# Low parts of 16 weight tiles of the second expert layer, made during the first layer's last sums and kept in DRAM

## The chip, the cores and the metric

The kernel runs on one NeuronCore of a Trainium2 chip. The metric is the time on the device of one execution, in microseconds (us). Of three runs the median was 2067.51 us (2065.51 to 2068.57). The profile is of one further execution, which took 2073.28 us.

## The reference, cut to what matters

256 tokens of width 1024 pass through two blocks. Each block is a token mixer and then an expert layer with 128 x 128 experts; the expert layer is the part that the change touches:

```python
def peer_2(xn, w_q, sub_keys, u_tab, v_tab):       # the first layer has the same shape
    q = (t @ w_q).reshape(n_tok, PEER_HEADS, 2, PEER_HALF)
    sc = jnp.einsum("thpk,hpnk->thpn", q, sub_keys)
    s_top, i_top = lax.top_k(sc, PEER_TOPK)         # 16 of 128, twice per head
    cand = s_top[:, :, 0, :, None] + s_top[:, :, 1, None, :]
    best, pos = lax.top_k(cand.reshape(n_tok, PEER_HEADS, kk), PEER_TOPK)
    g = jax.nn.softmax(best, axis=-1)
    act = jax.nn.gelu(einsum(u_tab[idx], t))        # chosen experts only
    return einsum(g * act, v_tab[idx])
```

Everything is float32. The kernel computes the products of all 16384 experts densely and multiplies by a gate that is zero for experts that were not chosen.

## The kernel before, in words

**Weights come as tiles of 128 x 1024 float32 (512 KB).** `plan` lists all tiles of the program in the order of their use; `fetch_to` loads them from SyncE's queue (SP) into three buffers named raw, at most three tiles ahead of the tile prepared last. A prepared tile is in two parts: `high` copies it on ScalarE (ACT) to a rounded format (whi, line 96), and `low` subtracts that copy on VectorE (DVE) to get the rest (wlo, line 103). Both parts have three buffers; `take` prepares two tiles ahead. TensorE (PE) then makes 24 matmuls for a tile, three for each of eight slices: high part by the high input, high part by the low input, low part by the high input (lines 137 to 139). The order of the instructions of every engine is the order of the program text; nothing reorders them.

**Whole tiles.** A tile marked "own" isn't split. It is loaded into three buffers of its own (rawf) and multiplied in float32 (line 131): 8 matmuls, each of which the trace records twice. In either expert layer ten of the tiles of `down` are whole: 5, 8, ..., 32.

**An expert layer** (`peer`) runs through five stages. (1) The lead: four tiles of the query weights (lead 0 to 3) are multiplied before the norm is known, while DVE and ACT make the norm; then one query tile and the first tile of `down`, q4 and S0, are multiplied together, slice by slice, as the normed input arrives (`norm_steps`). The keys (1 MB) are loaded here, between the preparation of q4 and that of S0 (line 1121). (2) Routing: the other queries q5 to q15 and the tiles S1 to S33 alternate on PE, and DVE works through the two top-16 searches, the decoding and the softmax, some 2 us behind each tile of `down` (a list of work items with estimated costs). The stage ends when DVE has written K and PE transposes it (line 1168); S32 and S33 stand behind the transposes. (3) The rest of the first 64 tiles of `down`, beside the gates. (4) The sums: for expert tile i of `up`, `weights(i + 1)` splits the gated activations (wh on ACT, line 122; wl on DVE, line 123), the tile i + 2 is prepared, and PE makes 24 matmuls (lines 1382 to 1384). Up to i = 47 a tile of `down` stands between two of `up`; from i = 48 on there are sums alone. (5) `finish` adds the result to x.

**Beside the last sums** of the first layer, from i = 66 on, the generator `before1` makes one step in each i. I call i - 65 the turn. Turns 1 to 5 make small sums and load the row crow; turn 7 works on crow (lines 315 to 317) and loads the first of eight rows aw; turns 9, 11, ..., 23 each multiply a row aw on DVE (`ada`, line 330) and load the next one, into the same single buffer.

Of the kernel before, what the change touches and what calls it, by code (L numbers as in the profile page):

```python
# [1 line left out]

# [6 lines left out]
F32 = _mybir.dt.float32  # L9
F32R = _mybir.dt.float32r  # L10
# [10 lines left out]
KT = 8  # L21
# [3 lines left out]
N0 = 34  # L25
# [26 lines left out]
class Net:  # L52
    def __init__(self, tc, a, out):
        self.tc, self.nc, self.a, self.out = tc, tc.nc, a, out
        self.items = []
        self.fetched = self.prepped = self.taken = 0

    def v(self, name, j=0, n=1):
# [23 lines left out]
    def high(self, n):  # L82

        it = self.items[n]
        if isinstance(it[3], tuple):
            return
        self.fetch_to(n + 1)
        if it[2]:
            it[3] = it[3],
            return  # L90
        if it[4]:
            hi, lo = self.extra
        else:
            hi = self.stream.tile([128, KT, 128], F32R, name="whi", bufs=3)
            lo = self.stream.tile([128, KT, 128], F32R, name="wlo", bufs=3)
        self.nc.scalar.copy(hi, it[3])  # L96
        it[3] = it[3], hi, lo

    def low(self, n):
        it = self.items[n]  # L100
# [5 lines left out]
    def prep_to(self, n):  # L106
        while self.prepped < min(n, len(self.items)):
            self.high(self.prepped)
            self.low(self.prepped)
            self.prepped += 1  # L110
            self.fetch_to(self.prepped + RAW)

    def take(self, key, index, prep=PREP):
        n = self.taken
        it = self.items[n]
        assert it[:2] == [key, index], (it[:2], key, index)
        self.prep_to(n + prep + 1)
        self.taken += 1
        return it[3]
# [918 lines left out]
            out.append(("U", n))  # L1038
        return out

    def plan_peer(self, wq, down, up):
        for st in self.peer_steps():
            if st[0] in ("q", "lead"):
                self.plan(wq, st[1], spare=st == ("lead", 1))
            elif st[0] in "SERH":

                self.plan(down, st[1], whole=4 < st[1] < N0 and st[1] % 3 == 2 and "own")
            elif st[0] == "U":
                self.plan(up, st[1], spare=st[1] == NK - 1)

    def peer(self, wq, keys, down, up, gelu, g, shift, before, finish):
        tc, nc, a = self.tc, self.nc, self.a
        steps = self.peer_steps()
        with self.sbuf("pk") as pk, self.psum("ps", 2) as self.pp, self.psum("pacc", 1) as pacc, \
# [8 lines left out]
            def S(i):  # L1063
                return self.proj(down, i, *([h] if self.items[self.taken][2] else [self.hh, self.hl]))

            with self.sbuf("rt") as rt:
# [8 lines left out]
                q = {}  # L1075
# [37 lines left out]
                lead = [acc[j].rearrange("p b t -> p (b t)")[:, :W] for j in range(4)]  # L1113
# [43 lines left out]
                n = 6  # L1157
# [46 lines left out]
            with self.sbuf("dn") as dn:  # L1204
# [3 lines left out]
                def gated(i):  # L1208
                    wf = X2[:, i - N1]
                    nc.vector.tensor_mul(wf, wf, acts.pop(i))  # L1210
# [3 lines left out]
                with self.sbuf("og") as og:  # L1214
# [89 lines left out]
                    first = []  # L1304
# [24 lines left out]
                    for m in range(ng + LAG):  # L1329
                        if m < ng:  # L1330
                            ahead_hots = one_hots(m + 2)
                            next(ahead_hots, None)
                            pool, tag = (self.pm, "sm") if m % 2 else (self.pp, "mm")
# [24 lines left out]
                        pass  # L1358
                n += N1 - N0 + RING + HELD + 1

                with self.sbuf("ga") as ga:
                    def act(i, ps):
                        g = ga.tile([128, T], F32, name="ge", bufs=2)
                        nc.scalar.activation(g, ps, gelu)
                        acts[i] = g
                        gated(i)

                    def weights(i):
                        if i >= NK:
                            return None  # L1370
                        wf = X1[:, i] if i < N1 else X2[:, i - N1]
                        wh = ga.tile([128, T], F32R, name="wh", bufs=2)
                        wl = ga.tile([128, T], F32R, name="wl", bufs=2)
                        self.split(wh, wl, wf)
                        return wh, wl

                    def bank(d):
                        return acc[d % 4][:, d // 4]

                    def spread_up(i, d, hi, lo, wh, wl):  # L1380
                        o = bank(d)
                        nc.tensor.matmul(o, hi[:, d], wh, start=i == 0 and d < 4, stop=False, skip_group_check=True)  # L1382
                        nc.tensor.matmul(o, hi[:, d], wl, start=False, stop=False, skip_group_check=True)  # L1383
                        nc.tensor.matmul(o, lo[:, d], wh, start=False, stop=i == NK - 1, skip_group_check=True)  # L1384

                    waiting = list(acts)
                    for i in held:
                        act(i, held[i])
                    w = weights(0)
                    for kind, i in steps[n:]:  # L1390
                        if waiting:
                            gated(waiting.pop(0))
                            if not waiting:
                                nc.gpsimd.dma_start(self.x, xk)
                        if kind == "S":
                            act(i, S(i))
                            continue
                        if i == N1 + 1:
                            x1.__exit__(None, None, None)
                            more = before()  # L1400
                        if i > N1 + 1:
                            next(more, None)
                        wc, w = w, weights(i + 1)
                        if i < NK - 2:
                            hi, lo = self.take(up, i)
                            for d in range(8):
                                spread_up(i, d, hi, lo, *wc)
                        elif i == NK - 2:
                            before_last = (*self.take(up, i), *wc)
                            self.prep_to(self.taken + 3)  # L1410
                        else:

                            hi, lo = self.take(up, i, prep=0)
                            for d in range(10):
                                if d < 8:
                                    spread_up(i - 1, d, *before_last)
                                if d > 1:
                                    spread_up(i, d - 2, hi, lo, *wc)
                                    finish(d - 2, bank(d - 2))

    def build(self):
        tc, nc, a = self.tc, self.nc, self.a
        self.plan_mixer1()
        self.plan_peer("w_query", "down", "up")
        self.plan_mixer2()
        self.plan_peer("w_query2", "down2", "up2")
        with tc.manual_schedule(), tc.tile_pool(name="const", bufs=1) as const, \
                tc.tile_pool(name="stream", bufs=2) as self.stream, \
                tc.tile_pool(name="np", bufs=1) as self.np, \
                tc.tile_pool(name="pm", bufs=2, space=PSUM) as self.pm:  # L1430
# [85 lines left out]
            def both_sums():  # L1516
# [5 lines left out]
                while True:  # L1522
# [1 line left out]

            self.mixer1(constants)
            self.peer("w_query", "keys", "down", "up", AF.Gelu, self.g1, self.mod[:, 24:32],
                      before1, first)
            self.mixer2(both_sums, g2)
            self.peer("w_query2", "keys2", "down2", "up2", AF.Gelu_apprx_tanh, self.v("norm2", 0, 8), None,
                      before2, second)  # L1530
# [91 lines left out]
```

## Time and profile before

| | |
|---|---|
| median of three runs | 2067.51 us |
| profiled execution, its span | 2073.28 us, 2071.5 us |
| busy: PE, DVE, ACT | 2002.1 us (97%), 1526.6 us (74%), 1057.1 us (51%) |
| one split of a tile: copy on ACT, subtraction on DVE | 1047 ns, 1224 ns, 599 of each |
| one split of gated activations: ACT, DVE | 404 ns, 422 ns, 256 of each |
| moved by DMA | 376.63 MB, 182 GB/s over the span |

In the profile PE, DVE and ACT are the shares of the span in which the engines were busy, DMA is the mean busy share of the 16 DMA engines, and a busy PE isn't PE at its peak, since matmuls overlap. The first expert layer ends at about 1025 us of the span, the lead of the second at about 1250, its routing at 1383.5.

### The profile page before, as it was taken

The page shows a single profiled execution, that of the slowest core. Times are in us where ns is not written, and L with a number is a line of the kernel's source. Part 1 is how long each engine was busy: PE and PEld are TensorE (multiplying, and loading weights), DVE is VectorE, ACT ScalarE, POOL GpSimd, SP SyncE. Part 2 cuts the span into 40 slices and gives each one's busy share as a digit, 9 for nine tenths or more (in the row PEclk, how much of TensorE's full clock was granted, in tenths as well). Part 3 has the DMA queues.
Part 4 walks back from the last instruction along what each step waited for, and adds up shares of the span by engine and source line. Part 5 has one row for each costly group of instructions (what it writes and reads, how often), then busy time and mean ns, then how long its engine had stood idle before and what let it go on. Part 6 is the DMA issues. An engine that isn't in the chain of part 4 may idle for free. (4 is left out here: it accounts for less than half of the span.)

```text
span 2071.5 us, 41220 instructions
## 1 busy us (share of the span) xinstructions
PE 2002.1 (97%) x16640; PEld 1955.9 (94%) x16640; DVE 1526.6 (74%) x3007; ACT 1057.1 (51%) x1986; POOL 51.9 (3%) x52
## 2 busy tenths in 40 slices
PE   5999999999999999999999999999999999999998
PEld 4888898999999999999999999999999999999998
DVE  7997899999655555665687779999996555555555
ACT  3453434666544444544575554446655444444444
POOL 3021000000000000000000010000000000000000
PEclk7999999999999999999999999999999999999999
DMA  8755444444555555675545564444445555555553
GB/s 300 261 203 185 161 164 153 143 142 141 198 190 186 184 186 191 209 243 190 184 153 183 183 215 172 155 153 143 143 144 201 185 184 187 189 185 186 190 184 123
DMA packets 102720, 376.63 MB, mean 182 GB/s; under 512 B 11648, under 2 KB 12032, under 8 KB 101504
## 3 DMA queue, kind: packets, MB, share of 16 engines
q1 hardware_dynamic: 101520, 369.38, 51.3%
q0 software_dynamic: 576, 4.19, 0.5%
q8 instruction: 130, 2.13, 0.4%
q14 instruction: 62, 0.51, 0.1%
q10 hardware_dynamic: 432, 0.41, 0.1%
HBM read 370.80 MB, written 3.15 MB: 181 GB/s over the span
## 5 line engine op out<-in xcount | busy, mean ns | idle before, releaser
L103 DVE TENSOR_TENSOR wlo<-raw,whi 128x1024 fp32r<-128x1024 f32 x599 | 732.4, 1224 | 248.6 <-ACT whi L96 247.3
L96 ACT CAST whi<-raw 128x1024 fp32r<-128x1024 f32 x599 | 626.4, 1047 | 238.8 <-PE acc L138 102.5
L1382 PE MATMUL acc<-wh,whi 128*128 128x256 f32 x2032 | 569.3, 280 | 2.1 <-DVE x L1494 2.1
L1384 PE MATMUL acc<-wh,wlo 128*128 128x256 f32 x2032 | 567.7, 279 | 2.2 <-DVE wlo L103 2.2
L1383 PE MATMUL acc<-wl,whi 128*128 128x256 f32 x2032 | 568.0, 280 | 1.7 <-DVE wl L123 1.3
L139 PE MATMUL mm<-hh,wlo 128*128 128x256 f32 x1880 | 530.0, 282 | 12.2 <-DVE wlo L103 12.2
L137 PE MATMUL mm<-hh,whi 128*128 128x256 f32 x1880 | 535.4, 285 | 3.3 <-ACT gg L879 1.4
L138 PE MATMUL mm<-hl,whi 128*128 128x256 f32 x1880 | 529.0, 281 | 2.9 <-DVE hl L258 2.1
L1384 PEld LDWEIGHTS acc<-wh,wlo 128*128 128x128 f32 x2032 | 381.9, 188 | 2.6 <-DVE wlo L103 2.6
L1382 PEld LDWEIGHTS acc<-wh,whi 128*128 128x128 f32 x2032 | 381.2, 188 | 2.4 <-DVE x L1494 2.3
L1383 PEld LDWEIGHTS acc<-wl,whi 128*128 128x128 f32 x2032 | 380.5, 187 | 3.0 <-DVE wl L123 2.9
L139 PEld LDWEIGHTS mm<-hh,wlo 128*128 128x128 f32 x1880 | 358.1, 190 | 16.0 <-DVE wlo L103 15.8
L137 PEld LDWEIGHTS mm<-hh,whi 128*128 128x128 f32 x1880 | 354.6, 189 | 6.4 <-ACT gg L879 1.8
L138 PEld LDWEIGHTS mm<-hl,whi 128*128 128x128 f32 x1880 | 356.0, 189 | 4.6 <-DVE hl L258 2.5
L122 ACT CAST wh<-X 128x256 fp32r<-128x256 f32 x256 | 103.4, 404 | 229.2 <-PE acc L1384 229.2
L137 PE MATMUL acc<-hh,whi 128*128 128x256 f32 x736 | 216.3, 294 | 0.0
L138 PE MATMUL acc<-hl,whi 128*128 128x256 f32 x736 | 205.3, 279 | 0.0
L139 PE MATMUL acc<-hh,wlo 128*128 128x256 f32 x736 | 204.8, 278 | 0.0
L123 DVE TENSOR_TENSOR wl<-X,wh 128x256 fp32r<-128x256 f32 x256 | 108.1, 422 | 89.1 <-ACT wh L122 89.1
L137 PEld LDWEIGHTS acc<-hh,whi 128*128 128x128 f32 x736 | 139.1, 189 | 0.0
L138 PEld LDWEIGHTS acc<-hl,whi 128*128 128x128 f32 x736 | 139.0, 189 | 0.0
L139 PEld LDWEIGHTS acc<-hh,wlo 128*128 128x128 f32 x736 | 138.4, 188 | 0.0
(343 smaller groups left out, 2136.3 us busy)
## 6 DMA issues: line engine op xcount, KB each, us to landing
raw<-in_up_dram SPq DMA_DIRECT2D x256, 512.0 KB, 3.4
raw<-in_down_dram SPq DMA_DIRECT2D x236, 512.0 KB, 3.2
raw<-in_w_in_dram SPq DMA_DIRECT2D x71, 512.0 KB, 3.3
aw<-in_w_ada_dram SPq DMA_DIRECT2D x48, 512.0 KB, 4.6
raw<-in_w_query_dram SPq DMA_DIRECT2D x32, 512.0 KB, 3.3
rawf<-in_down_dram SPq DMA_DIRECT2D x20, 512.0 KB, 4.4
rawf<-in_w_in_dram SPq DMA_DIRECT2D x10, 512.0 KB, 4.6
raw<-in_w_out_dram SPq DMA_DIRECT2D x8, 512.0 KB, 3.8
```

What stands on the lines that cost most here:

```text
L96: self.nc.scalar.copy(hi, it[3])
L103: self.nc.vector.tensor_sub(lo, raw, hi.bitcast(F32))
L122: self.nc.scalar.copy(hi, src)
L123: self.nc.vector.tensor_sub(lo, src, hi.bitcast(F32))
L137: nc.tensor.matmul(ps, hi[:, k], xh[:, k], start=k == 0 and clear, stop=False, skip_group_check=True)
L138: nc.tensor.matmul(ps, hi[:, k], xl[:, k], start=False, stop=False, skip_group_check=True)
L139: nc.tensor.matmul(ps, lo[:, k], xh[:, k], start=False, stop=k == KT - 1, skip_group_check=True)
L1382: nc.tensor.matmul(o, hi[:, d], wh, start=i == 0 and d < 4, stop=False, skip_group_check=True)
L1383: nc.tensor.matmul(o, hi[:, d], wl, start=False, stop=False, skip_group_check=True)
L1384: nc.tensor.matmul(o, lo[:, d], wh, start=False, stop=i == NK - 1, skip_group_check=True)
```

## The change

In the second layer no tile is whole any more. The low parts of 16 of its tiles (lead 0 to 3, q4, S0 and the ten that were whole) are made during the last sums of the first layer, from turn 1 on: a tile is loaded, copied to a high part on ACT and subtracted on DVE in place, and the difference is stored by a DMA from ACT's queue to a buffer in DRAM. Each tile takes two steps of the new generator, one for the copy (and the store of the tile before), one for the subtraction; a step is made in turns 1 to 7 and from then on in every odd turn. The load of a tile stands one step before its copy for the first, and beside the copy of the tile before for the others. In the second layer these 16 tiles are loaded and copied to a high part as the others are, and the low part is a load from DRAM on SP's queue instead of the subtraction on DVE.

```diff
@@ high(self, n)
         self.nc.scalar.copy(hi, it[3])
-        it[3] = it[3], hi, lo
+        if n in self.early:
+            self.nc.sync.dma_start(lo.bitcast(F32), self.early[n])
+            it[3] = hi, lo
+        else:
+            it[3] = it[3], hi, lo
+    def lows_ahead(self, pool, home, items):
+        nc = self.nc
+        raws, done = {}, None
+        def load(m):
+            if m < len(items):
+                key, index = self.items[items[m]][:2]
+                raws[m] = pool.tile([128, KT, 128], F32, name="early", bufs=3)
+                nc.sync.dma_start(raws[m], self.a[key][index])
+        load(0)
+        for m, n in enumerate(items):
+            yield
+            load(m + 1)
+            raw = raws.pop(m)
+            hi = pool.tile([128, KT, 128], F32R, name="ehi", bufs=1)
+            nc.scalar.copy(hi, raw)
+            if done:
+                nc.scalar.dma_start(*done)
+            yield
+            nc.vector.tensor_sub(raw.bitcast(F32R), raw, hi.bitcast(F32))
+            self.early[n] = home.tile([128, KT, 128], F32, name=f"lo{n}")
+            done = self.early[n], raw
+        nc.scalar.dma_start(*done)
@@ plan_peer(self, wq, down, up, first)
+            if not first and (st[0] == "lead" or st in (("q", 4), ("S", 0))
+                              or st[0] == "S" and 4 < st[1] < N0 and st[1] % 3 == 2):
+                self.ahead.append(len(self.items))
-                self.plan(down, st[1], whole=4 < st[1] < N0 and st[1] % 3 == 2 and "own")
+                self.plan(down, st[1], whole=first and 4 < st[1] < N0 and st[1] % 3 == 2 and "own")
@@ peer(...), the last sums
                         if i == N1 + 1:
                             x1.__exit__(None, None, None)
                             more = before()
+                            lows, turn = iter(()), 0
+                            if home:
+                                lows = self.lows_ahead(later.enter_context(self.sbuf("el")), home, self.ahead)
                         if i > N1 + 1:
                             next(more, None)
+                            turn += 1
+                            if turn % 2 or turn < 8:
+                                next(lows, None)
                         wc, w = w, weights(i + 1)
```

## Rows read from the trace of the kernel before

**Rows 1.** Busy time by stretch: engines with instructions, granted TensorE clock, DMA share, GB/s.
```profile
1250.50:1383.40 132.90, 127.91 (x967) 122.70 (x965) 131.96 (x491) 52.77 (x89) 0.00 (x0) 1.00 0.47 167
1240.00:1245.00 5.00, 5.00 (x33) 4.93 (x32) 3.91 (x10) 2.57 (x5) 0.00 (x0) 0.72 0.46 157
849.00:869.00 20.00, 19.69 (x168) 19.48 (x166) 13.25 (x31) 11.39 (x17) 0.00 (x0) 1.00 0.60 211
869.00:916.00 47.00, 45.87 (x383) 45.20 (x384) 34.34 (x50) 21.80 (x32) 0.00 (x0) 1.00 0.81 261
920.00:1020.00 100.00, 100.00 (x852) 100.00 (x851) 58.34 (x72) 48.06 (x71) 0.00 (x0) 1.00 0.54 188
8.00:18.00 10.00, 5.25 (x32) 5.16 (x32) 6.99 (x6) 5.61 (x13) 8.39 (x3) 0.63 1.01 405
```

**Rows 2.** Groups of instructions by line and form, routing of the second layer, 1250.5 to 1383.4.
```profile
L103 DVE TENSOR_TENSOR wlo<-raw,whi 128x1024 fp32r<-128x1024 f32 x31 | 37.6, 1214 | 0.0
...
L131 PE MATMUL mm<-h,rawf 128*128 128x256 f32 x144 | 32.6, 379 | 0.0
```

**Rows 3.** The chain that ended last, at the end of that routing: start, duration, what.
```profile
1384.30 3.46 PE mm L131 x16
1387.76 0.12 PE mm L137
...
1390.59 0.12 PE acc L137
```

**Rows 4.** PE in order of time in the second lead: start, duration, what, [idle before].
```profile
1238.42 0.39 PE L139 MATMUL mm<-hh,wlo 128*128 128x256 f32 x1 [0.76 <-DVE wlo L103]
...
1240.18 0.41 PE L137 MATMUL mm<-hh,whi 128*128 128x256 f32 x1
1240.40 0.41 PE L138 MATMUL mm<-hl,whi 128*128 128x256 f32 x1
...
1245.47 0.39 PE L138 MATMUL mm<-hl,whi 128*128 128x256 f32 x1 [0.34 <-DVE hl L261]
```

**Rows 5.** ACT in the same lead: copies of lead 2 and 3, q4, S0.
```profile
1227.00 1.98 ACT L96 CAST whi<-raw 128x1024 fp32r<-128x1024 f32 x2
1229.94 1.05 ACT L96 CAST whi<-raw 128x1024 fp32r<-128x1024 f32 x1 [0.96 <-PE acc L138]
...
1236.07 1.04 ACT L96 CAST whi<-raw 128x1024 fp32r<-128x1024 f32 x1
```

**Rows 6.** SP's queue in the same lead.
```profile
1229.32 5.35 SPq L79 DMA_DIRECT2D raw<-in_down_dram  x3
1234.72 0.42 SPq L1121 DMA_DIRECT2D keys<-in_keys_dram  x1
```

**Rows 7.** PE in order of time in the first layer's last sums.
```profile
869.35 0.39 PE L1383 MATMUL acc<-wl,whi 128*128 128x256 f32 x1 [0.66 <-DVE wl L123]
...
910.43 0.39 PE L1383 MATMUL acc<-wl,whi 128*128 128x256 f32 x1 [0.27 <-DVE wl L123]
```

**Rows 8.** DVE in the same sums: crow in turn 7, first and last of eight aw.
```profile
867.74 1.23 DVE L317 SCALAR_TENSOR_TENSOR crow<-aw,crow 128x1024 f32<-128x1024 f32 x1 [2.17 <-ACT crow L316]
...
872.33 1.23 DVE L330 SCALAR_TENSOR_TENSOR aw<-aw,crow 128x1024 f32<-128x1024 f32 x1 [0.42 <-DMA aw<-in_w_ada_dram]
...
914.41 1.23 DVE L330 SCALAR_TENSOR_TENSOR aw<-aw,crow 128x1024 f32<-128x1024 f32 x1 [0.35 <-DMA aw<-in_w_ada_dram]
```

**Rows 9.** ACT in the same sums, turns 6 and 7.
```profile
862.96 0.41 ACT L122 CAST wh<-X 128x256 fp32r<-128x256 f32 x1 [1.47 <-PE acc L1384]
...
865.55 1.06 ACT L315 ACTIVATE aw<-crow 128x1024 f32<-128x1024 f32 x1 [1.24 <-DMA crow<-in_c_dram]
```

**Rows 10.** Loads of crow on SP's queue there.
```profile
860.33 0.63 SPq L311 DMA_DIRECT2D crow<-in_c_dram  x1
```

**Rows 11.** From issue to landing: raw at 920 to 1020, aw at 869 to 916.
```profile
DMA to landing us min/median/max: 3.1/3.2/4.9
DMA to landing us min/median/max: 3.2/4.5/5.4
```

More of the change, by code (lines that the diff above doesn't have):

```diff
@@ L1 @@
+import contextlib
 import numpy as _np
@@ L55, in __init__ @@
         self.items = []
+        self.early = {}
         self.fetched = self.prepped = self.taken = 0
@@ L1039, in peer_steps, with plan_peer @@
         return out
-    def plan_peer(self, wq, down, up):
+    def plan_peer(self, wq, down, up, first):
         for st in self.peer_steps():
+            if not first and (st[0] == "lead" or st in (("q", 4), ("S", 0))
+                              or st[0] == "S" and 4 < st[1] < N0 and st[1] % 3 == 2):
+                self.ahead.append(len(self.items))
             if st[0] in ("q", "lead"):
@@ L1045, in plan_peer, with peer @@
             elif st[0] in "SERH":
-                self.plan(down, st[1], whole=4 < st[1] < N0 and st[1] % 3 == 2 and "own")
+                self.plan(down, st[1], whole=first and 4 < st[1] < N0 and st[1] % 3 == 2 and "own")
             elif st[0] == "U":
                 self.plan(up, st[1], spare=st[1] == NK - 1)
-    def peer(self, wq, keys, down, up, gelu, g, shift, before, finish):
+    def peer(self, wq, keys, down, up, gelu, g, shift, before, finish, home=None):
         tc, nc, a = self.tc, self.nc, self.a
@@ L1359, in peer @@
                 n += N1 - N0 + RING + HELD + 1
-                with self.sbuf("ga") as ga:
+                with self.sbuf("ga") as ga, contextlib.ExitStack() as later:
                     def act(i, ps):
@@ L1423, in build @@
         self.plan_mixer1()
-        self.plan_peer("w_query", "down", "up")
+        self.ahead = []
+        self.plan_peer("w_query", "down", "up", True)
         self.plan_mixer2()
-        self.plan_peer("w_query2", "down2", "up2")
+        self.plan_peer("w_query2", "down2", "up2", False)
         with tc.manual_schedule(), tc.tile_pool(name="const", bufs=1) as const, \
+                tc.tile_pool(name="lows", bufs=1, space=bass.MemoryType.DRAM) as lows, \
                 tc.tile_pool(name="stream", bufs=2) as self.stream, \
@@ L1526, in build @@
             self.peer("w_query", "keys", "down", "up", AF.Gelu, self.g1, self.mod[:, 24:32],
-                      before1, first)
+                      before1, first, lows)
             self.mixer2(both_sums, g2)
```

## The prediction

> **What bounds the kernel now.** I began with the busy time by stretch, since one share over the whole span mixes stages. In the second layer's routing DVE is busy 131.96 of 132.90 us and PE 127.91 [rows 1]: DVE ends that stage, and PE has 4.99 us to spare. In the last sums of the first layer it is the other way round: at 920 to 1020 us PE is busy all the time, DVE 58.34 of 100 us and ACT 48.06, with the DMA engines at 0.54 [rows 1]. Just before that, while the rows aw are worked on, PE already loses time (45.87 of 47.00) and DMA is at 0.81 and 261 GB/s [rows 1]. The groups by line then say what DVE does in the routing: 31 subtractions of 1214 ns for the split tiles, and none for the whole ones, of which PE has 144 records, nine tiles of 16 [rows 2]. The chain shows what PE pays for one whole tile, 3.46 us (1384.30 to 1387.76), and for the split tile after it, 24 matmuls from 1387.76 to 1390.59, 2.83 us [rows 3].
>
> **Part 1: no whole tiles in the routing.** PE saves 3.46 - 2.83 = 0.63 us a tile, 5.7 us for the nine in the routing. But whole tiles cost DVE nothing, and the new ones cost it nothing either: its 31 subtractions and all its search work remain. Nine tiles faster on PE only make PE wait longer for DVE. The gain is at most DVE's own idle time, 132.90 - 131.96 = 0.94 us, and I take 0. If the low parts from DRAM came late by 1 us each, PE would use 9 of the 4.99 + 5.7 = 10.7 us that it then has; no cost either. ACT gets ten copies of 1.05 us, beside 52.77 us busy of 132.90; ten loads of 0.524 MB add 39 GB/s to 167. The tenth whole tile, S32, stands behind the transposes, where the chain is on PE [rows 3]: -0.6 us, between -0.7 and 0.
>
> **Part 2: the lead of the second layer.** Six subtractions of about 1.22 us go. Five of them cost PE nothing. That of S0 does: PE waited 0.76 us for it, until 1238.42 [rows 4], as its copy began only at 1236.07 [rows 5]. In its place stands a load, and the question is when it lands. SP's queue before had three loads of raw from 1229.32 on and then the keys at 1234.72 [rows 6], each raw waiting for DVE's subtraction of an older tile. Now a raw waits for a copy only, so the queue moves up: raw S0 at about 1228.0, where the first of two copies from 1227.00 ends, low part 3, raw S1 at 1229.0, low part of q4, raw S2 at 1231.0 (the copy of 1229.94 plus 1.05) [rows 5], the keys, and behind them the low part of S0. That is 6 x 0.524 + 1.05 = 4.19 MB. With nothing else on the queue a raw lands 3.2 us after its issue [rows 11]; 0.524 MB at the 405 GB/s that the engines moved at share 1.01 [rows 1] are 1.3 us of it, which leaves 1.9. So the low part of S0 lands at 1228.0 + 1.9 + 4.19/0.405 = 1240.2, or at 1243.0 with 322 GB/s (261 at share 0.81, scaled to 1 [rows 1]). PE is 1.8 to 4.6 us later there than before, minus the 0.34 that it lost later in waiting for DVE's hl at 1245.47 [rows 4] and as much for the earlier gaps: DVE makes the normed input earlier now. Routing starts when PE has finished the pair and S1, so this shifts everything behind it. If the engines serve the queue otherwise and the load lands by 1237.4, PE gains about 1 us there and another at hl: -2. I take +2.0, between -2 and +5.
> The clock matters here too. In 1240 to 1245, after PE had waited, the granted clock was 0.72, with matmuls 0.22 us apart (1240.18 to 1240.40) instead of 2.83/24 = 0.118 [rows 1, 3, 4]. Of two levels, 2.4 and 1.2 GHz, that is 2.8 of 5 us at the lower, and 1.4 us lost. A longer wait brings this again, or somewhat more; it is inside the upper end.
> The Trainium skill ("DMA: Bandwidth & Descriptors", Specifications) gives about 358 GB/s as the limit of a core's HBM. By it the low part of S0 would land at 1241.6 and the term would be 1.4 us larger, an estimate. The trace differs, 405 GB/s over 10 us [rows 1], and the trace decides.
>
> **Part 3: the work beside the last sums of the first layer.** Added are 16 loads and 16 stores of 0.524 MB, 16 copies of 1.05 us on ACT, 16 subtractions of 1.22 us on DVE. PE takes 2.83 us for one i.
> Turns 1 to 8. ACT is idle 1.47 us before each wh [rows 9], which waits for PE; a copy fits in if its tile has landed. But the loads of the first tiles are issued only one or two turns ahead. The first one stands right behind a raw, as crow does at 860.33 in turn 5 [rows 10]; it lands 3.2 to 4.0 us on, then come the copy 1.05, wh 0.41, wl 0.42 and some 0.2 between them: 5.3 to 6.1 us, where PE wants wl after two i, 5.7. With two later copies I take +1.0 (0 to 2.5). In turn 7 DVE works on crow from 867.74, wl stands behind that, and PE waited 0.66 for it [rows 7, 8]. A subtraction now stands between: +1.1. ACT had waited 1.24 us for the load of crow [rows 9]; in turns 1 to 7 four loads and two stores, 3.1 MB in 20 us or 157 GB/s, join 211 [rows 1], so crow lands one transfer later, +1.3 (0 to 2.6). Sum 3.4, between 1 and 6.
> Turns 9 to 23. From 872.33 to 914.41 seven rounds took 42.08 us, 6.01 each [rows 8], where two i on PE take 5.66: a round is the 4.5 us that aw needs to land [rows 11], the 1.23 on DVE and the issue. wl stands behind it, and PE was waiting for wl [rows 7]: there is no slack left. In four rounds of eight a store now runs beside the load of aw. At 405 GB/s it takes 1.3 us from the engines; two thirds of it fall on aw, +0.9 each, 3.6. In the other four a subtraction stands between aw and wl. The next aw is issued before it, so it doesn't lengthen the round; PE loses its 1.1 once. Sum 4.7. Below, 1.1: the stores hide. Above, 9: by volume 261 GB/s x 47 us + 8 x 0.524 MB = 16.5 MB, at 322 GB/s 51.2 us instead of 47, and the raws late on top.
> The Trainium skill ("DMA: Bandwidth & Descriptors", Issuing engines are not separate DMA queues) says that transfers started from different engines run on the same 16 DMA engines and interleave, so a second queue saves issue time alone. No row here shows a store beside loads. By that rule the 3.6 stand; with a separate path for ACT's queue that term would be 0.
> Turns 25 to 59. Nine tiles are left, with no aw: DVE gets 11 us on 58, DMA goes from 188 to 281 GB/s [rows 1]. Loads are four turns ahead. 0, up to 2. Part 3 in all: +8.1, between 2 and 17.
>
> **Sum.** -0.6 + 2.0 + 8.1 = +9.5 us. Against the profiled execution, 2073.28 us (span 2071.5 and 1.8 around it), that is 2082.8. That execution lies 5.8 us above the median of the runs; I assume that the difference stays and add the 9.5 to 2067.51: 2077.
>
> **Rivals.**
> (a) *The work beside the sums is hidden.* For: DVE, ACT and DMA are half idle there [rows 1]. Against: PE waits for wl behind aw already [rows 7]. Part 3 is then 0 to 2, part 2 about -1.5: some 2066.
> (b) *Routing gets shorter: faster.* If PE and not DVE ended the routing, nine tiles would give 5.7, S32 0.6, and the lead 2.0: 8.3 minus 2 for the sums, 2061. For: PE is on the chain at its end [rows 3]. Against: DVE's 131.96 us of work remain; it decides from the point at which 1250.5 to 1383.4 takes less than 132 us.
> (c) *DMA becomes the bound beside the sums and in the lead.* The upper ends: -0.6 + 4 + 14 = +17, 2085. For: 0.81 share before, with 350 GB/s wanted [rows 1]. Against: 405 GB/s shown at another place.
>
> **How the numbers follow.** The forecast 0.55 (2070 to 2082), (a) 0.20, (b) 0.07, (c) 0.18. What can be told from no change is 0.2%, 4.1 us: 2063.4 to 2071.6. Slower: 0.53 + 0.18 = 0.71; same 0.22, 0.19 of it (a); faster 0.07, 0.06 of it (b). The range leaves out (b), the fastest part of (a) and the slowest of (c): 2066 to 2088.
>
> **What would show it.** Part 1: DVE's busy time from the first search to K still about 132 us, PE's fallen by some 6, its waits for wlo in the routing above 10 instead of about 5. Part 2: the matmul on S0's low part waiting for a DMA, later than 1238.4 by the clock of its stage. Part 3: more than 2 us of waits of PE for wl in turns 7 and 8, and about 1 us more in each second round of aw, the landing of aw at 5 to 6 us in half of them. The prediction is wrong if the first layer's sums end at the same time as before, or if the routing takes fewer than 131 us.

## The result and the profile after

The changed kernel took 2078.56 us (median of six runs, 2076.09 to 2083.20), the kernel before in the same comparison 2067.84 (2062.68 to 2068.94). The ratio is 1.0076, 95% interval 1.0058 to 1.0095: 12.0 to 19.6 us slower, in the middle 15.7. The two medians alone are 10.7 us apart. So the forecast of 2077 us and its range hold the time, but of the loss it had only 9.5 us. The profiled execution took 2080.64 us (span 2078.8).

Busy time by stretch in the changed kernel (columns as in [rows 1]): the routing, the rows aw, the sums without aw, the end of the lead.

```profile
1262.50:1396.20 133.70, 125.14 (x1041) 123.21 (x1039) 132.29 (x490) 61.57 (x98) 0.00 (x0) 0.99 0.57 198
...
869.00:922.00 53.00, 49.13 (x390) 48.52 (x391) 39.64 (x54) 25.27 (x36) 0.00 (x0) 0.95 0.91 315
925.00:1020.00 95.00, 95.00 (x809) 95.00 (x808) 63.59 (x76) 53.43 (x75) 0.00 (x0) 1.00 0.80 277
...
1246.00:1256.00 10.00, 6.37 (x31) 5.97 (x30) 7.04 (x18) 3.81 (x8) 0.00 (x0) 0.69 0.59 230
```

Against [rows 1]: in the routing DVE is as busy as before and PE has more idle time (8.56 us, before 4.99), and the stage is not shorter. Beside the aw, DMA went from 0.81 to 0.91 and PE loses 3.87 of 53 us at a clock of 0.95. Without aw PE is still busy all the time, at 277 GB/s.

ACT in order of time, turns 2 to 7 (it answers to [rows 9]; start, duration, what, [idle before]):

```profile
848.14 1.05 ACT L137 CAST ehi<-early 128x1024 fp32r<-128x1024 f32 x1 [3.48 <-DMA early<-in_w_query_dram]
849.09 0.40 ACT L155 CAST wh<-X 128x256 fp32r<-128x256 f32 x1
...
853.39 1.05 ACT L137 CAST ehi<-early 128x1024 fp32r<-128x1024 f32 x1 [1.69 <-DVE early L141]
...
860.11 1.05 ACT L137 CAST ehi<-early 128x1024 fp32r<-128x1024 f32 x1 [2.03 <-DMA early<-in_w_query_dram]
...
863.96 1.06 ACT L348 ACTIVATE aw<-crow 128x1024 f32<-128x1024 f32 x1 [1.55 <-DMA crow<-in_c_dram]
```

and PE there, in the second lead and behind the routing (they answer to [rows 4, 7]; the last is S32):

```profile
849.54 0.38 PE L1418 MATMUL acc<-wh,whi 128*128 128x256 f32 x1 [0.63 <-ACT wh L155]
853.71 0.39 PE L1419 MATMUL acc<-wl,whi 128*128 128x256 f32 x1 [0.61 <-DVE wl L156]
866.46 0.39 PE L1418 MATMUL acc<-wh,whi 128*128 128x256 f32 x1 [1.14 <-ACT wh L155]
868.89 0.58 PE L1419 MATMUL acc<-wl,whi 128*128 128x256 f32 x1 [2.05 <-DVE wl L156]
...
1231.67 0.39 PE L172 MATMUL acc<-gh,wlo 128*128 128x256 f32 x1 [0.61 <-DMA wlo<-lo]
1234.22 0.39 PE L172 MATMUL acc<-gh,xlo 128*128 128x256 f32 x1 [1.93 <-DMA xlo<-lo]
1250.45 0.58 PE L172 MATMUL mm<-hh,wlo 128*128 128x256 f32 x1 [3.34 <-DMA wlo<-lo]
...
1398.12 0.38 PE L172 MATMUL mm<-hh,wlo 128*128 128x256 f32 x1 [0.72 <-DMA wlo<-lo]
```

At 849.54 the chain is a copy on ACT that waits for its load, wh behind the copy, PE behind wh. At 866.46 wh stands behind crow, which waits for its own load. The two waits for wl have another cause: wh is long done, and wl stands behind a subtraction of an early tile, in the longer one behind crow and a subtraction. DVE there (it answers to [rows 8]):

```profile
866.14 1.22 DVE L350 SCALAR_TENSOR_TENSOR crow<-aw,crow 128x1024 f32<-128x1024 f32 x1 [2.47 <-ACT crow L349]
867.29 1.22 DVE L141 TENSOR_TENSOR early<-early,ehi 128x1024 fp32r<-128x1024 f32 x1
868.42 0.42 DVE L156 TENSOR_TENSOR wl<-X,wh 128x256 fp32r<-128x256 f32 x1
```

In the lead PE waits 5.9 us for low parts from DRAM where it had waited 0.76 us for DVE's of S0 [rows 4].

SP's queue in that lead (it answers to [rows 6]):

```profile
1226.70 0.41 SPq L101 DMA_DIRECT2D xlo<-lo  x1
...
1234.62 0.33 SPq L82 DMA_DIRECT2D raw<-in_down_dram  x1
...
1236.30 0.76 SPq L82 DMA_DIRECT2D raw<-in_down_dram  x1
1239.69 0.33 SPq L101 DMA_DIRECT2D wlo<-lo  x1
1240.65 0.33 SPq L82 DMA_DIRECT2D raw<-in_down_dram  x1
1241.03 0.42 SPq L1157 DMA_DIRECT2D keys<-in_keys_dram  x1
1242.77 0.33 SPq L101 DMA_DIRECT2D wlo<-lo  x1
```

S0's low part is issued at 1242.77, behind the keys, and used at 1250.45.

**A table by stage.** The products on hh between two of the sums are 117.7 ns apart in some executions and 113.5 ns in others, of either kernel (last section); it moves both stretches of 270.3 us to 265.7 us. So I compare lengths of stages, between the starts of PE instructions of each profile: the first matmul of i = 64, 76, 92 and 124 of the first sums, of the second lead and of its scores, and from there to the last K on DVE.

| profile | 64-76 | 76-92 | 92-124 | 124-lead | lead-scores | scores-K |
|---|---|---|---|---|---|---|
| before, first / again | 34.85 / 33.92 | 46.89 / 45.23 | 90.45 | 208.9 | 25.17 | 132.8 |
| change, first / again | 42.35 / 41.54 | 49.90 / 51.82 | 90.45 | 210.5 / 210.4 | 30.80 / 29.44 | 133.5 / 134.0 |
| make only | 41.95 | 51.30 | 90.45 | 205.1 | 25.21 | 132.8 |
| routing's lows | 40.96 | 50.28 | 90.45 | 210.7 | 25.18 | 127.6 |
| make from turn 9 | 35.83 | 50.47 | 90.45 | 212.0 | 25.16 | 132.8 |
| the same, no stores | 37.49 | 48.64 | 90.45 | 211.9 | 25.17 | 132.8 |
| to turn 8, loads ahead | 38.28 | 45.91 | 90.45 | 208.9 | 25.18 | 132.8 |
| use only | 37.62 | 45.96 | 92.29 | 208.9 | 30.59 | 133.5 |
| keys later | 36.45 | 45.23 | 90.45 | 208.9 | 27.15 | 135.5 |
| after the aw | 35.89 | 47.11 | 108.00 | 210.2 | 28.86 | 132.6 |
| nine late | 35.45 | 45.24 | 90.45 | 211.8 | 25.18 | 127.6 |
| seven late | 37.84 | 46.01 | 90.45 | 210.2 | 25.15 | 128.3 |

Without a step there, 64-76 takes 33.9 to 37.8 (seven profiles, mean 36.0); 76-92 takes 45.2 to 47.1 without steps or with the first of turns 25 and 26 alone (eight profiles, mean 46.0); with all steps (four profiles) 41.7 and 50.8. The change is 5.7 + 4.8 + 1.5 + 5.0 + 0.9 = 17.9 us by these stages, inside both measured intervals (that of the change again stands below).

**The clock is a part of it.** The whole stage 64-76 before, in the change, and with the loads ahead (columns as in [rows 1]):

```profile
842.97:877.82 34.85, 34.19 (x290) 33.98 (x289) 24.14 (x46) 18.21 (x26) 0.00 (x0) 1.00 0.63 217
837.44:879.79 42.35, 37.85 (x290) 36.74 (x289) 27.36 (x50) 21.91 (x30) 0.00 (x0) 0.92 0.80 283
838.12:876.40 38.28, 35.26 (x291) 34.24 (x289) 27.26 (x49) 21.16 (x29) 0.00 (x0) 1.00 0.75 272
```

A mean clock of 0.92 over 42.35 us is 3.4 us lost, beside some 4.4 us of waits of PE. Over the four profiles with all steps PE waits 3.9 to 4.7 us in 64-76 and the clock takes 1.7 or 3.4; without a step the waits are 0 to 2.0 us (mean 1.2) and the clock takes 1.7 in two profiles of the seven and nothing in the others.

### The profile page after: what moved, and what is told of

The parts are those of the page before. It is cut to its first block, busy times and chain, and to the rows that moved or that the text cites. A ratio compares the mean times of both kernels' runs of the same rounds, so it can differ in the third digit from the quotient of the medians.

```text
span 2078.8 us, 41512 instructions
## 1 busy us (share of the span) xinstructions
PE 1997.3 (96%) x16720; PEld 1955.1 (94%) x16720; DVE 1535.8 (74%) x3017; ACT 1082.5 (52%) x2012; POOL 51.9 (2%) x52
## 3 DMA queue, kind: packets, MB, share of 16 engines
q0 software_dynamic: 576, 4.19, 0.5%
## 4 chain that ended last, share of the span: by engine, by line
PE 71%; DVE 10%; DMA 3%; ACT 3%; issue 3%; DVEq 0%; ACTq 0%; SPq 0%
PE acc L1419 11%; PE acc L1418 11%; PE acc L1420 11%; PE mm L172 8%; PE mm L170 8%; PE mm L171 8%; PE acc L170 4%; PE acc L171 3%; PE acc L172 3%; DVE wlo L110 3%; PE mm L1374 2%; ACT whi L99 2%; PE sm L1374 2%; DMA wlo<-lo 1%; DVE I L998 1%
## 5 line engine op out<-in xcount | busy, mean ns | idle before, releaser
L99 ACT CAST whi<-raw 128x1024 fp32r<-128x1024 f32 x609 | 637.7, 1048 | 245.0 <-PE acc L171 105.3
L172 PE MATMUL mm<-hh,wlo 128*128 128x256 f32 x1960 | 552.1, 282 | 17.5 <-DMA wlo<-lo 9.5
L170 PE MATMUL mm<-hh,whi 128*128 128x256 f32 x1960 | 557.0, 284 | 3.3 <-ACT gg L912 1.4
L171 PE MATMUL mm<-hl,whi 128*128 128x256 f32 x1960 | 550.6, 281 | 1.2 <-DVE hl L291 1.0
L172 PEld LDWEIGHTS mm<-hh,wlo 128*128 128x128 f32 x1960 | 373.3, 190 | 21.3 <-DMA wlo<-lo 10.7
L170 PEld LDWEIGHTS mm<-hh,whi 128*128 128x128 f32 x1960 | 373.2, 190 | 6.3 <-ACT gg L912 1.8
L171 PEld LDWEIGHTS mm<-hl,whi 128*128 128x128 f32 x1960 | 374.0, 191 | 2.3 <-DVE hl L291 1.4
L155 ACT CAST wh<-X 128x256 fp32r<-128x256 f32 x256 | 103.3, 403 | 213.7 <-PE acc L1420 210.7
```

The lines of the kernel that those rows point to most:

```text
L155: self.nc.scalar.copy(hi, src)
L170: nc.tensor.matmul(ps, hi[:, k], xh[:, k], start=k == 0 and clear, stop=False, skip_group_check=True)
L171: nc.tensor.matmul(ps, hi[:, k], xl[:, k], start=False, stop=False, skip_group_check=True)
L172: nc.tensor.matmul(ps, lo[:, k], xh[:, k], start=False, stop=k == KT - 1, skip_group_check=True)
```

## The experiments

My theory A: most of the loss is made beside the first sums, where loads, copies and subtractions collide with crow and aw; the rest in the second lead; the routing is bound by DVE. Rival B: it is made in the second layer. The kernels are told by their changes against the changed kernel. Ratios are against the kernel before in the same comparison; its own median went from 2063.67 to 2072.23 us between comparisons.

**The two halves, and the change again.**

```diff
 make only
-        if n in self.early:
+        if False:
-   whole=first and 4 < st[1] < N0 ...
+   whole=4 < st[1] < N0 ...
 use only (one low part made, in turns 25 on)
-        if n in self.early:
+        if n in self.ahead:
-            self.nc.sync.dma_start(lo.bitcast(F32), self.early[n])
+            self.nc.sync.dma_start(lo.bitcast(F32), self.early[self.ahead[0]])
```

> The 16 low parts are made and stored beside the first layer's last sums exactly as in the changed kernel, but the second layer doesn't use them: it splits its tiles on DVE and keeps its ten whole tiles, as the kernel before. Theory A (most of the loss is made beside the first sums, by loads, copies, subtractions and stores that collide with crow and aw): the time is 8 to 12 us above the kernel before, the last sums (turn 1 to the end of the first layer) about 10 us longer, the second layer as before. Rival B (the loss comes in the second layer's lead and routing, where low parts arrive by DMA): 0 to 3 us above the kernel before.

> Only one low part is made (turns 25 to 27), and the second layer loads this one buffer 16 times where the changed kernel loads 16 different ones; whole tiles are gone as in the changed kernel. The second layer's instructions are those of the changed kernel, only the first layer's extra work is left out. Theory A: 4 to 6 us above the kernel before, all of it in the second lead (PE waits about 2 us for the low part of lead 1 and 3 us for that of S0, and routing starts 5 to 6 us late), the routing itself within 1 us of before (132 to 134 us). Rival B: nearly the whole loss of the change, 9 to 11 us. Rival (routing bound by PE): the routing 3 to 6 us shorter and the time at or below the kernel before.

> The changed kernel itself once more, beside the others of this group. Theory A, now by the sum of its two halves (make only: last sums 11.4 us longer by the stage clock, 7.5 us at the end; use only: lead 2.6 us, from there to the scores 2.8 us, routing 0.7 us longer): 12 to 18 us above the kernel before. If the halves hide one another (a PE wait that stands in both is paid once): 9 to 12 us.

Make only: ratio 1.0047 (1.0034 to 1.0060), 7.0 to 12.4 us. Use only: 1.0046 (1.0031 to 1.0062), 6.4 to 12.8. The change again: 1.0093 (1.0068 to 1.0118), 14.0 to 24.4. So the halves add up, and neither B nor "paid once" stands. By the times alone the halves are equal, which would be against A's "most"; by stages A holds: of the change's 17.9 us, 12.0 lie before the second lead and 5.9 in lead and routing. Use only costs more than the 4 to 6 that I expected because its time has parts of the first layer in it: lead and routing give 6.1 us by stages, its one low part, with a step in each of turns 25 to 27, 1.8 in 92-124, and 64-76, where it has no step, is 1.6 above the mean. Of make only, 124-lead is 205.1 us where others have 208.9 with the same instructions: the shorter spacing stood in the middle of that stage alone (its second layer takes 270.35 us again), which makes the end of that stage (7.6 us later) look better than its sums. The lead in use only, what PE waits for (us in total, times, longest):

```profile
PE mm L172 <- DMA wlo<-lo: 3.7, 1, 3.7
PE acc L172 <- DMA xlo<-lo: 1.9, 1, 1.9
PE acc L172 <- DMA wlo<-lo: 0.4, 1, 0.4
```

It is the lead of the change, without its first layer: the waits belong to the low parts' loads.

**Steps after the aw alone.**

```diff
-                            if turn % 2 or turn < 8:
+                            if turn > 24:
```

> The same 16 low parts, but the first step comes in turn 25 and a step in every turn from there to turn 57, so that nothing stands beside crow and the rows aw; everything else as in the changed kernel. Theory A (the cost comes from the collision with crow and aw in turns 1 to 23): the first layer's sums end within 2 us of before, the time is 4 to 6 us above the kernel before, which is the lead's part. Rival C (16 loads, stores, copies and subtractions cost PE the same wherever they stand, as volume): 9 to 12 us above, and with a step in each turn the aw-free turns become 8 to 10 us longer.

1.0110 (1.0093 to 1.0128): 23 us slower, more than the change. 64-92 is as without steps, but 92-124 takes 108.00 us. The early tiles in that stretch, and the stretch:

```profile
  DMA early<-in_down_dram: 27.7, 8
  DMA early<-in_w_query_dram: 13.4, 4
...
DMA to landing us min/median/max: 3.6/6.2/7.6
```
```profile
925.00:1030.00 105.00, 94.62 (x744) 90.00 (x745) 66.95 (x79) 56.26 (x78) 0.00 (x0) 0.98 0.87 301
```

ACT's copies waited 41.1 us for loads that land after 6.2 us, where a tile is wanted every two i (5.66 us). What was wanted is a raw each 2.83 us and a load and a store each 5.66: 4 x 0.524 MB in 5.66 us, 370 GB/s; it moved 301. At half that pace (the change, 277 GB/s) the same stretch loses nothing. Both theories missed this: place is not enough. In turns 1 to 7 steps come as fast. But a load is issued two turns ahead at this pace and four at the other, so whether the bytes or the late issue decides isn't shown: no run has this pace with earlier loads.

**Which turns, and which part of a step.**

```diff
 make from turn 9 (make only, 13 tiles)
-                            if turn % 2 or turn < 8:
+                            if turn % 2 and turn > 8:
 the same without stores: of the 13 only the last low part is stored
-            if done:
-                nc.scalar.dma_start(*done)
 to turn 8, loads ahead (make only, 3 tiles, all loads in turn 1)
-        load(0)
+        for m in range(3):
+            load(m)
-            load(m + 1)
-                            if turn % 2 or turn < 8:
+                            if turn in (1, 3, 4, 5, 6, 7, 8):
```

> Make only, but the steps stand in the odd turns from 9 on alone (13 low parts; turns 1 to 7 are as in the kernel before); the second layer doesn't use them and keeps its whole tiles. Theory A (the cost has two places, 6 to 7 us in turns 1 to 8, where a load must land in two turns, and 3 to 4.5 us beside the rows aw): the sums end 3 to 5 us later than before, the time is 2.5 to 5 us above. Rival (the late start of crow and the fall of the clock in turns 6 to 10 are what costs, and the rows aw alone are absorbed): 0 to 2 us above. Rival (beside the aw DMA alone is the bound): 9 us or more, as with all steps.

> As the make-only kernel with steps from turn 9 on (13 tiles), but the low parts are not stored (one of them is, at the end): loads, copies and subtractions alone. Theory A (beside the rows aw the stores cost most, 3.6 of 4.7 us, as they share the DMA engines with the aw loads): from i = 72 to i = 92 the sums take 1 to 2 us longer than before instead of 4.6. Rival (the loads of the early tiles do it, or the subtractions between aw and wl): 3.5 to 4.6 us longer, as with the stores.

> Make only, three low parts in turns 1 to 8 alone: all three loads are issued in turn 1, the copies stand in turns 3, 5 and 7 and the subtractions in turns 4, 6 and 8; no step later. Nothing is used in the second layer. Theory A (the cost of turns 1 to 8, about 6.8 us as the difference of all steps and of those from turn 9 on, comes from copies on ACT that wait for a load issued only two turns before, with wh and wl queued behind them): the waits of ACT for early loads fall from 7.4 us to under 2, the sums end 1 to 3 us later than before. Rival (crow's later landing and the subtraction in turn 7 do it, and DMA's volume): 5 to 7 us later, as the loads now stand still closer to crow's.

From turn 9: 1.0045 (1.0030 to 1.0060), 9.3 us where A said 2.5 to 5; 76-92 is 4.5 us longer, 64-76 not, so the aw cost is not absorbed and doesn't need the steps before. The third expectation has the time right and the place wrong: in 124-lead 3.1 us are lost, of them a wait of 1.2 us for wh in its last turns and a fall of the clock. In their times this kernel and make only (1.0047) can't be told apart; what turns 1 to 8 add in make only and the change rests on the stages. Without stores: 1.0042 (1.0025 to 1.0059), no difference in time; 76-92 is still 2.7 us longer. From i = 72, where the expectation counts, it takes 63.52 us to 92, with stores 63.68, as the rival said, though a fall of the clock (1.7 us) stands in the first alone. So the stores are 1.8 of 4.5 us at most, from one profile of each kernel, and loads, copies and subtractions the larger part. What PE waits for at 845 to 945, without stores, and then with:

```profile
PE acc L1418 <- DVE wl L155: 3.3, 5, 0.9
PE acc L1417 <- ACT wh L154: 0.6, 1, 0.6
```
```profile
PE acc L1419 <- DVE wl L156: 3.7, 4, 1.3
PE acc L1418 <- ACT wh L155: 1.5, 2, 1.1
```

and both stretches beside the aw, in the same order:

```profile
862.00:925.00 63.00, 59.15 (x478) 57.92 (x477) 47.26 (x64) 33.84 (x48) 0.00 (x0) 0.97 0.79 276
862.00:925.00 63.00, 57.73 (x476) 56.31 (x475) 46.13 (x62) 34.35 (x49) 0.00 (x0) 1.00 0.89 299
```

Loads ahead: 1.0024 (1.0007 to 1.0040). ACT's waits for early tiles fall to 0.7 us (7.4 in make only, 5.5 in the change), as these rows of its ACT say, and 64-76 is 2.3 us longer instead of 5.7:

```profile
ACT aw L348 <- DMA crow<-in_c_dram: 2.8, 1, 2.8
...
ACT ehi L137 <- DMA early<-in_w_query_dram: 0.7, 1, 0.7
```

So A's forecast holds, but the kernel differs in more than the lead of its loads: it has three loads instead of four in these turns, and the subtraction that stood behind crow in turn 7 stands in turn 8, with a copy in its place. PE's waits are some 1.6 us shorter than with all steps (2.7 for 4.3), and no clock is lost there (2.1 on average with all steps); how much of that is the copies' waiting for their loads isn't shown. What is left is crow, which ACT now waits for 2.8 us (before 1.24 [rows 9]).

**The keys behind S0's low part** (use only, and in the second layer):

```diff
+                if home:
                     nc.sync.dma_start(kt, a[keys])
                 ...
                 self.prep_to(self.taken + 2)
+                if not home:
+                    nc.sync.dma_start(kt, a[keys])
```

> As the use-only kernel (one low part made, in turns 25 to 29, and loaded 16 times), but the load of the 1 MB of keys of the second layer stands behind the loads of S0's low part and of the raws on SP's queue, not ahead of them. Theory A (S0's low part is late because the keys' 1.05 MB are ahead of it): PE's wait of 3.7 us for that low part falls to 0.5 to 1.5 us, and the scores start 2 to 3 us earlier against the start of the lead than in the use-only kernel. Rival (the load can't be issued before its buffer is free and lands too late from there, whatever is ahead of it): the wait stays at 3 us or more. The wait of 1.9 us for the low part of lead 1 stays in both.

1.0025 (1.0010 to 1.0040). PE in its lead:

```profile
PE acc L172 <- DMA xlo<-lo: 2.3, 1, 2.3
PE mm L171 <- DVE hl L294: 0.7, 1, 0.7
PE mm L172 <- DMA wlo<-lo: 0.4, 1, 0.4
```

The wait for S0's low part (3.7 us) is gone, 0.7 us for hl is late next, and lead-scores falls by 3.4 us: theory A. Up to half of the 3.4 can be a shorter fall of the clock in the lead (1.7 us lost there, 3.4 in use only). But scores-K grew by 2.0 us, so K comes only 1.5 us earlier. In that stage DVE, which bounds it, waits 3.7 us for ACT (0.4 in use only), and the clock fell twice (once in use only). Use only and keys later there:

```profile
1258.10:1392.50 134.40, 125.64 (x1050) 123.71 (x1049) 132.96 (x491) 62.08 (x99) 0.00 (x0) 0.99 0.57 196
1245.70:1382.10 136.40, 127.57 (x1050) 125.60 (x1048) 133.33 (x492) 62.06 (x99) 0.00 (x0) 0.97 0.57 194
```

**What bounds the routing.** Six split tiles of the routing get early low parts in place of lead 0 to 3, q4 and S0:

```diff
-            if not first and (st[0] == "lead" or st in (("q", 4), ("S", 0)) or ...
+            if not first and st[0] == "S" and (
+                    4 < st[1] < N0 and st[1] % 3 == 2 or 6 < st[1] < 23 and st[1] % 3 == 1):
```

> 16 other tiles get early low parts: the ten formerly whole ones and six split tiles of the routing (S7, S10, S13, S16, S19, S22); lead 0 to 3, q4 and S0 are split on DVE as in the kernel before. The work in the first layer is as in the changed kernel. Theory A (DVE ends the routing): DVE loses six subtractions of 1.21 us, the routing gets 6 to 7.5 us shorter than before (125.5 to 127 us), the lead is within 1 us of before, the first sums 8 to 11 us longer: 1 to 4 us above the kernel before. Rival (PE or the arriving low parts end the routing): the routing stays at 131 to 134 us and the time is 8 to 11 us above the kernel before.

1.0029 (1.0019 to 1.0039), the first layer as slow as in the change, the lead as before, scores-K 127.6 us: 5.2 less. The time is 6.0 us above before, more than A's 1 to 4, as the first layer loses 11 us by stages. DVE and PE in the routing:

```profile
1260.99:1387.99 127.00, 122.64 (x1038) 120.84 (x1037) 124.80 (x485) 60.68 (x97) 0.00 (x0) 1.00 0.66 232
```

DVE bounds the routing: with the same ten whole tiles gone, it gets shorter only once subtractions go. It gives 5.2 of the 7.3 us of six subtractions; DVE is idle 2.2 us now.

**Versions from these readings:** low parts only for routing tiles, steps only in odd turns after the aw, the other whole tiles kept.

```diff
-                            if turn % 2 or turn < 8:
+                            if turn > 24 and turn % 2:
+NINE = 6, 12, 14, 18, 20, 24, 26, 30, 32      (or SEVEN = 6, 12, 18, 20, 24, 30, 32)
-            if not first and (st[0] == "lead" or ...
+            if not first and st[0] == "S" and st[1] in NINE:
```

> A version that follows from the readings: only nine low parts are made, with a step in each odd turn from 25 to 61, when no aw is left and DMA has room; they are those of S6, S12, S18, S24, S30 (split before) and S14, S20, S26, S32 (whole before); the other six whole tiles stay whole and the lead is that of the kernel before. Theory A: the first sums and the lead end within 1 us of before, DVE loses five subtractions of 1.21 us in the routing, which takes 126 to 128 us instead of 132.9: 4.5 to 6.5 us below the kernel before. Rival 1 (the routing is bound by PE or by arriving low parts): within 2 us of before. Rival 2 (loads and stores beside the aw-free turns cost PE too): up to 4 us above before.

> As the version with nine low parts, but seven: S6, S12, S18, S24, S30 (split before) and S20, S32 (whole before), with a step in each odd turn from 25 to 53, so that the last twelve i of the first sums are as before. Theory A: the searches and what follows up to K take 126 to 127.5 us instead of 131.6 (five subtractions fewer on DVE), the end of the sums loses nothing (the version with nine lost 1.4 us there): 3 to 5.5 us below the kernel before. Rival 1 (PE, with fewer whole tiles replaced, ends the routing): 1 to 2 us below. Rival 2 (what the routing gives is lost elsewhere again): within 1 us of before.

Nine: 1.0000 (0.9985 to 1.0015). Seven: 0.9987 (0.9973 to 1.0001), medians 2060.61 and 2063.67. The routing does what A says for nine (127.6 us) and nearly for seven (128.3), with no loss in 92-124, yet the time shows 0 and 2.7 us of it, the second with an interval that reaches no change. In the profiles 124-lead is 2.9 and 1.3 us longer (nine: steps up to turn 61, and a fall of the clock in both), and 64-76 of the second 3.5 us longer than before's mean, with no step there (1.7 of it a fall of the clock). Whether those two are chance or belong to the versions stays open; rival 2 is excluded for neither.

**The kernel before against itself.**

> The kernel before, timed against itself and profiled once more. Theory (the spacing of the matmuls on hh between two of the sums, 117.7 ns in some runs and 113.5 ns in others, and falls of the granted clock that cost about 1.5 us each, come with a run and not with a kernel): the ratio is 1 within 0.0015, the spacing is one of the two values in both layers, and stages differ from the first profile by 0 to 2 us where a fall of the clock stands in one of them only. Rival (the spacing belongs to a kernel): 117.7 ns again, as in the first profile.

1.0009 (0.9994 to 1.0023), and the other spacing: 113.5 ns, with 265.65 us for either stretch of 270.3. So the spacing is no mark of a kernel. The stage 64-92 was 79.15 us after 81.74 in the first profile, more than the 0 to 2 expected and with no fall of the clock in either: 2.6 us there are no difference.

## Why the prediction was right or wrong

**Part 1, right.** DVE is busy 132.29 of 133.70 us, as the text had it (about 132), and nine faster tiles only made PE wait: 8.3 us for low parts (5.5 for DMA, 2.8 for DVE) where it said above 10. It shows in the changed kernel and again, from the other side, in the experiment with the routing's lows. Two small terms were off. The routing is 0.7 to 1.2 us longer, not 0. By scores-K that goes with the clock: 133.5, 134.0 and, in use only, 133.5 with one fall in it, 135.5 with two (keys later), 132.6 with none (after the aw). And S32's 0.63 us went into 0.72 us of waiting for its low part (the row at 1398.12).

**Part 2, right place, mis-sized: +2.0 forecast, 4.3 to 5.6 measured.** S0's low part was late behind the keys, as described, and moving the keys removes that wait. The size failed in two terms. "Five of them cost PE nothing" is wrong for lead 1, whose low part was issued at 1226.70 and wanted by 1232.3; PE waited 1.93 us, and 0.61 for another. And "4.19 MB" at 405 GB/s was too little at too high a rate. The head of the queue did move up as worked out: raw S0 was issued at 1234.62, which is 1228.05 on the clock of before (the lead starts 6.57 us later), 1228.0 in the sum. From there S0's low part took 15.8 us, where the sum has 12.2:

```profile
1234.60:1250.40 15.80, 12.22 (x102) 11.76 (x100) 8.21 (x29) 6.46 (x13) 0.00 (x0) 0.98 0.97 377
...
1232.95 0.58 POOL L1188 DMA_DIRECT2D xk<-x  x1
...
SPq L101 <- PE acc L172: 3.8, 2, 2.5
```

The DMA engines are busy 0.97 and move 6.0 MB. Of the copy xk, 1 MB that GpSimd's queue issues just before, nearly all falls into this stretch, and the sum didn't have it; loads issued earlier were still in flight too. In the queue two low parts waited 3.8 us for buffers that PE still read and held up what stood behind them, so the keys came at 1241.03 and S0's low part at 1242.77, 7.7 us before its use. What each of these is worth isn't shown. The landing of 1240.2 becomes 1250.45 - 6.57 = 1243.9 on the clock of before, above even the 1243.0 by the lower rate. The clock stood at 0.69 in 1246 to 1256, 6.2 us at the lower level and 3.1 lost, where I had 1.4.

**Part 3, turns 1 to 8: +3.4 forecast, 5.7 measured,** inside 1 to 6. The term for the subtraction in turn 7 (+1.1) is borne out: the longest wait, 2.05 us, is for a wl that the subtraction holds up by 1.13 us (867.29 to 868.42). What the sum put at nothing there is the clock: the falls behind those waits take 1.7 or 3.4 us with all steps, on average 1.6 more than without a step, and PE's waits are some 3.1 longer; 1.0 of the 5.7 stays open. The term "copies that wait for their loads", +1.0, is of the right kind (0.63 us at 849.54), but no run isolates it. The loads were said to land in 3.2 to 4.0 us; among others in flight they took 2.8 to 6.7, median 5.0. The text saw the chain (copy, wh, wl, PE) and put the landing of an idle queue into it. A second reason that it did not have is the single buffer ehi (1.69 us at 853.39).

**Turns 9 to 23: +4.7 forecast, 4.8 measured, and that is luck in part.** "Stores 3.6, subtraction 1.1" is at most 1.8, and 2.7 or more for what is left without stores, loads and copies included. The landing of aw did go to a median of 5.0 us (4.5 before [rows 11]), and the DMA engines' share beside the aw is 0.89 with stores and 0.79 without. The Trainium skill ("DMA: Bandwidth & Descriptors", Issuing engines are not separate DMA queues) says that transfers from different issuing engines run on the same 16 DMA engines, and these two shares agree.

**Turns 25 to 59: 0, right to the row:** 90.45 us from i = 92 to 124 in both kernels.

**What was not in the sum:** 1.5 us between the sums and the second lead. The clock is 0.66 in 1030 to 1035 of the changed kernel, and 1.0 there in the kernel before. Except make only, every kernel that makes seven or more low parts has such a fall there; the others have none.

Of the rivals, (a) and (b) are out. (c), DMA as the bound in both places with +17 us, comes nearest in size: 17.9 by stages. In the lead its mechanism is near what the runs show (DMA share 0.97); beside the sums it isn't shown. The forecast had the places of the two large losses right and half of their sum. It priced waits of PE and, but for the lead, no fall of the clock behind them. That the time came out 1.6 us from 2077 is luck: the medians of that comparison lie 10.7 us apart, where its ratio gives 15.7 and the second comparison 19.2.

## What to carry to other kernels

Work that fits into an engine's idle share costs time if an in-order queue has it wait: issue its load as early as the landing time among other transfers needs, not the landing time of an idle queue, and mind its pace (277 GB/s with loads four turns ahead were free here, 370 asked for with loads two turns ahead were not). Add to the price of a wait of PE the fall of the clock that may follow it. A value fetched from memory instead of computed needs a place in the load queue ahead of whatever is wanted later, and its buffer free by then. Before taking work from one engine in a stage, look up which engine is saturated there: whole tiles were free for DVE, and only its own subtractions shortened the routing.

## What the runs showed of the hardware

The products on hh between two of the sums had a spacing that changed between executions of one kernel. Two profiles of the kernel before, the same 216 us of the first layer (groups by line and form):

```profile
L1382 PE MATMUL acc<-wh,whi 128*128 128x256 f32 x307 | 86.0, 280 | 0.0
L139 PE MATMUL mm<-hh,wlo 128*128 128x256 f32 x306 | 85.9, 281 | 0.0
```
```profile
L1382 PE MATMUL acc<-wh,whi 128*128 128x256 f32 x311 | 86.8, 279 | 0.0
L139 PE MATMUL mm<-hh,wlo 128*128 128x256 f32 x312 | 86.2, 276 | 0.0
```

In the second, four and six more of these matmuls pass in the same time: those on hh follow at 113.5 ns instead of 117.7, those of the sums stay at 117.7, at a granted clock of 1.00 in both. Over two layers that is 9.4 us, as much as the forecast change. It can change within an execution too: in make only both stretches take 270.35 us, and in 1105 to 1180 us, between them, the products on hh are 114.0 ns apart on average where both profiles of the kernel before have 117.4. Why is open.

And the granted clock fell to its lower level for a few us in every profile, at places that differ between executions of one kernel. Between 830 and 2000 us each of these falls, 34 in 14 profiles, stands at a wait of PE of 0.76 to 4.16 us; but not every such wait has one, as 2.07 us at 1025.21 in the first profile of the kernel before. In 124-lead, five profiles with one fall and PE's waits as before take 1.2 to 1.8 us more than 208.9.
